# Loading the second half of the token rows into weight and filter buffers, and transposing them among the filter units

## The chip, the cores and the metric

One core of a Trainium2 chip runs the kernel. The metric is the device time of one execution in microseconds (us); the median of three runs of the kernel before is 1380.2 us (1378.26 to 1383.59).

## The reference, cut to what matters

One transformer block on 1024 tokens of width 1024, with a context of 256 tokens. In float32:

```python
x = x + pos_embed
mod_x, mod_c = split(silu(c) @ w_ada + b_ada, 6), split(silu(c_ctx) @ w_ada + b_ada, 6)
def project(h, mod):
    return modulate(rmsnorm(h, norm_mix_g), mod[0], mod[1]) @ w_in   # q, k, v, g, decay gates, hyena inputs
# gated linear attention over the context, then over the tokens, both directions
# hyena: 3-tap convolution, then two long convolutions by FFT with filters made from
#   h = sin(freq * (sin(freq * (z @ w1 + b1)) @ w2 + b2)) @ w3, times a decay
x = x + mod_x[2] * (concat(gla, hyena) @ w_out)
x = x + mod_x[5] * expert_choice_moe(modulate(rmsnorm(x, norm_ffn_g), mod_x[3], mod_x[4]))   # 16 experts
return rmsnorm(x, norm_final_g)
```

The change lies in the beginning: the token rows (`x` plus position embedding, normalised and modulated), the first third of `mod_x`, and the spectra of the hyena filters.

## The kernel before, in words

The kernel is one straight program over five compute engines. Who computes what: TensorE (PE) multiplies, VectorE (DVE) and ScalarE (ACT) do elementwise work, GpSimd (POOL) and SyncE (SP) mostly issue transfers. The source is traced from top to bottom; a planner then sets the order of each engine and each queue. It takes the earliest source line that it reckons to be ready and to have a free buffer, by its own estimate of durations. On the chip each engine and each queue then works strictly in that order, and waits where a needed result or a transfer is later than reckoned.

Buffers are slots shared by tag. The ones that matter here:

- `gen`, 7 slots of 4 KB a partition: the features `zf`, the layers `h1` and `h2`, the split filter weights `w3` (two) and `h2h`, and the token rows `xt`. The last three of the former stay until the filter units are through, so four slots are left for token rows.
- `raw`, 3 slots: raw blocks of `w_in` (`w_block`, L508 to L520) and, later, pieces of `w_ada`.
- `whi` and `wlo`, 3 slots each: the two halves of a split `w_in` block, and before that the two halves `kk` of a filter unit (L453).
- `wa`, 8 slots: the first third of `w_ada`.

The beginning, in the order of the source:

1. Small loads on SP (L207 to L223): `w1`, `zf`, then the three columns `fb` (two biases and the frequency), `w2`, the condition columns, `w3raw`. Two sine layers make `h2` from them (L240 to L255).
2. `rows_of` (L279 to L309) for the first four row tiles of `x`: load, add the position embedding with DVE, sum of squares on ACT (L300, into `jk`), `rsqrt`, scale (L305).
3. `mod_begin` (L318) loads `b_ada` into `mo` with eight small transfers on SP; `mod_piece` (L326) streams 16 tiles `wt` of `w_ada` of 512 KB each and multiplies them; `mod_end` (L338) stores a third with four transfers on POOL. The first third is not stored but transposed into columns `mcol` and `g1` (L347 to L356).
4. Small loads on SP for later stages: `wab` and `pre` (L566 to L572), `cw` and `cb` (L644 to L648).
5. `columns` (L496) transposes four row tiles to `xh` and `xl`, with the modulation applied. L640 does it for the first half of the rows. L641 does all of the second half: `rows_of` with `by_dma`, in which SP loads `xt` and POOL adds the position embedding to it by an accumulating transfer (L288, L290), and then its transposes.
6. The same for the 256 context rows (L732 to L734).
7. `filters` (L476): eight units. `filter_front` multiplies and makes `kk`, with a small load `hb` on POOL (L457); `filter_mid` does the first DFT stage (L461 to L471); `filter_end` does the rest on DVE and stores `d_spec` on POOL (L474). A unit's front runs one unit ahead of its mid. After units 5 and 7 stand `value_rows` 0 and 1, whose `short_conv` (L650) multiplies a `w_in` block with both halves of `xh` and `xl`.
8. Gates, context projection and context states, and then the eight long-convolution slots, each with projections and pieces of `w_ada` among them.

In `rows_of`, the lines that matter most for the change are:

```python
xt = gen([P, D], name="xt")
SY.dma_start(xt, src[j * P:(j + 1) * P, :])
if by_dma:
    G.dma_start(xt, io["c_pos"][j], accum_op=ALU.add)
```

Of the kernel before, what the change touches and what calls it, by code (L numbers as in the profile page):

```python
# [98 lines left out]
def tile_gla_hyena_moe(ctx: ExitStack, tc: tile.TileContext, io: dict, out: bass.AP):  # L99
# [34 lines left out]
    def cload(name, shape, dt=F32, pool=None, src=None):  # L134
        t = (pool or const).tile(shape, dt, name=name)
        SY.dma_start(t, io["c_" + name] if src is None else src)
        return t
# [52 lines left out]
    def gen(shape, dt=F32, name="gen"):  # L190
        return gp.tile(shape, dt, name=name, tag="gen", bufs=7)
# [4 lines left out]
    def raw_tile(shape, name="raw"):  # L196
        return wp.tile(shape, F32, name=name, tag="raw", bufs=3)
# [6 lines left out]
    def twice(src, ap):  # L204
        return bass.AP(tensor=src.tensor, offset=src.offset, ap=ap)

    SY.dma_start(w1, twice(io["hy_w1"], [[DK, 33], [0, 2], [1, DK]]))  # L207
    zf = gen([33, L], name="zf")
    SY.dma_start(zf, io["c_zfeat"])
    for i, nm in enumerate(("hy_b1", "hy_b2", "hy_freq")):  # L210
        SY.dma_start(fb[:, i:i + 1], twice(io[nm], [[0, 2], [1, DK], [1, 1]]))
    SY.dma_start(w2, twice(io["hy_w2"], [[DK, DK], [0, 2], [1, DK]]))
    ccol = early.tile([P, KT, 2], F32, name="ccol")
    SY.dma_start(ccol[:, :, 0], io["c"][0].rearrange("(k p) -> p k", p=P))
# [61 lines left out]
    ident = cload("ident", [P, P])  # L276


    def rows_of(src, h, W, with_pos, by_dma=False):  # L279
        if with_pos and not by_dma:  # L280
            posc = s2([P, 512], name="posc")
            SY.dma_start(posc, io["c_posc"])
        xs_ = []
        ms = tiny.tile([P, W], F32, name="pms")
        for w in range(W):
            j = h * W + w
            xt = gen([P, D], name="xt")
            SY.dma_start(xt, src[j * P:(j + 1) * P, :])  # L288
            if by_dma:
                G.dma_start(xt, io["c_pos"][j], accum_op=ALU.add)  # L290
            elif with_pos:
                pr = s2([P, 512], name="posr")
                for q in range(2):
                    row = io["c_posr"][2 * j + q]
                    SY.dma_start(pr[64 * q:64 * q + 64],
                                 bass.AP(tensor=row.tensor, offset=row.offset, ap=[[0, 64], [1, 512]]))
                V.tensor_add(xt[:, 0:512], xt[:, 0:512], pr)
                V.tensor_add(xt[:, 512:1024], xt[:, 512:1024], posc)
            jk = s2([P, D], BF16, name="jk")
            A.activation(jk, xt, AF.Square, accum_out=ms[:, w:w + 1])  # L300
            xs_.append(xt)
        rs = tiny.tile([P, W], F32, name="prs")
        rsqrt(rs, ms, float(D), W)
        for w in range(W):
            A.activation(xs_[w], xs_[w], AF.Copy, scale=rs[:, w:w + 1])  # L305
        return xs_
# [5 lines left out]

    wav = w_ada.rearrange("(k p) (t h f) -> t k h p f", p=P, h=2, f=1024)

    def mod_columns(rows, t, g):
        return rows[:, 2048 * t:2048 * t + 2048].rearrange("r (h g j) -> r g h j", h=2, g=4)[:, g]

    def mod_begin(t, pool):  # L318
        mo = pool.tile([P, 512], F32, name="mo", tag="mo", bufs=1)
        G.memset(mo, 0.0)  # L320
        for g in range(4):
            for i in range(2):
                SY.dma_start(mo[32 * g + i:32 * g + i + 1].rearrange("r (h j) -> r h j", h=2), mod_columns(io["b_ada"], t, g))
        return mo

    def mod_piece(t, kqs, mo, raw):  # L326
# [9 lines left out]
        return V.tensor_add(mo, pm, mo)  # L336

    def mod_end(t, mo):  # L338
        for g in range(4):
            G.dma_start(mod_columns(d_mod, t, g), mo[32 * g:32 * g + 2].rearrange("r (h j) -> r h j", h=2))  # L340

    mo = mod_begin(0, early)
    mod_piece(0, range(4), mo, lambda shape, name: wap.tile(shape, F32, name=name, tag="wa", bufs=8))
    gcol = early.tile([P, KT], F32, name="gcol")
    SY.dma_start(gcol, io["norm_mix_g"][0].rearrange("(k p) -> p k", p=P))
    mcol = early.tile([P, 2, 2, KT], F32, name="mcol")
# [218 lines left out]

    wab = early.tile([65, NH, 2, DK], F32, name="wab")  # L566
    V.memset(wab, 0.0)
    for d, x in enumerate("fb"):
        for r in (0, 32):
            SY.dma_start(wab[r + 16 * d:r + 16 * d + 16, :, d], io["gla_wa_" + x][0].rearrange("r (h k) -> r h k", h=NH))  # L570
        SY.dma_start(wab[64:65, :, d], io["gla_ba_" + x].rearrange("r (h k) -> r h k", h=NH))
    pre = cload("pre", [P, 2 * (CH + 2)], pool=early)  # L572
    sgn = early.tile([P, 2], F32, name="sgn")
    for x in range(2):
        V.memset(sgn[0:64, x:x + 1], 1.0 - 2.0 * x)
# [62 lines left out]
    xh = [xpool.tile([P, L], F32R, name=f"xh{k}") for k in range(KT)]  # L638
    xl = [xpool.tile([P, L], F32R, name=f"xl{k}") for k in range(KT)]
    columns(first_rows, 0, 0, xh, xl)  # L640
    columns(rows_of(io["x"][0], 1, 4, True, True), 1, 0, xh, xl)  # L641


    cw = early.tile([P, 12, 3], F32, name="cw")  # L644
    for j in range(3):
        SY.dma_start(cw[:, :, j], io["hy_conv_w"][0, j].rearrange("(b p) -> p b", p=P))
    cb = early.tile([P, 12], F32, name="cb")
    SY.dma_start(cb, io["hy_conv_b"][0].rearrange("(b p) -> p b", p=P))  # L648

    def short_conv(b, depth=3):  # L650
        ps = pA([P, L], name="phy")
# [162 lines left out]
    def value_rows(b, depth=3):  # L814
        u = short_conv(b, depth)
        uts[(0, b)] = to_time_rows(lambda n1: u[:, n1::8])

    filters(decay0, {5: lambda: value_rows(0, 2), 7: lambda: value_rows(1, 2)})
    hl = gate_weights()
    context_gates(hl)  # L820
    block_a(hl)
# [626 lines left out]
```

## Time and profile before

| what | value |
| --- | --- |
| median of 3 runs | 1380.2 us |
| the profiled execution, its own time | 1380.59 us |
| its span, first to last instruction | 1378.8 us |
| PE busy | 1276.7 us (93% of the span) |
| DVE busy | 1149.8 us (83%) |
| ACT busy | 805.8 us (58%) |
| POOL busy | 129.9 us (9%) |
| mean granted TensorE clock | 0.964 |
| moved by DMA | 354.81 MB, mean 257 GB/s |

Busy time is an average over stages with different limits, so it says where to look and not what a change is worth. A row of a stage table gives, for one stretch of time, how long each engine was busy in it, the granted clock of TensorE (1.00 is 2.4 GHz, 0.50 is 1.2 GHz) and the share of time in which the 16 DMA engines worked. A row of a timeline gives start, duration, engine, line, and operation, and in brackets how long the engine had been idle and what ended that. SPq is SP's queue of transfers. In a row of the timeline the duration of SPq is the time that issuing takes, not the time until the data is there.

### The profile page before, as it was taken

The numbers are of one execution on the slowest core, as the hardware profiler recorded it, in microseconds if no ns is written. First come the engines' busy times: TensorE is split into PE (matmuls) and PEld (weight loads), VectorE is DVE, ScalarE is ACT, GpSimd is POOL, SyncE is SP. The second block draws the span as 40 slices with busy tenths as digits, with TensorE's granted clock in tenths as the row PEclk, the third lists the DMA queues.
The fourth block names the chain that finished last, engine by engine and source line by source line (L and its number), as shares of the span: only waits on it lengthen the run. The fifth ranks groups of instructions, "written<-read, shape, count | busy, mean of one in ns | idle before, by whom it ended". The sixth has DMA issues, their size and how long they took to land.

```text
span 1378.8 us, 21543 instructions
## 1 busy us (share of the span) xinstructions
PE 1276.7 (93%) x7720; PEld 1044.5 (76%) x7720; DVE 1149.8 (83%) x1920; ACT 805.8 (58%) x1228; POOL 129.9 (9%) x142
## 2 busy tenths in 40 slices
PE   6988999999999998988996899999999999999982
PEld 4777888688898897766775678888888888877762
DVE  6877938899778678788656799999999999988886
ACT  3247453121211314886553678888888888877864
POOL 1020000010100110001000000001111111012010
PEclk9998999999999998999996899999999999999996
DMA  7993551774746545676768789999999999999765
GB/s 213 325 230 123 167 145 42 234 199 150 202 152 185 141 113 176 159 165 186 242 230 337 244 318 357 361 394 383 387 385 386 390 385 391 369 365 370 264 202 225
DMA packets 154362, 354.81 MB, mean 257 GB/s; under 512 B 28389, under 2 KB 74013, under 8 KB 153999
## 3 DMA queue, kind: packets, MB, share of 16 engines
q1 hardware_dynamic: 134911, 292.84, 59.7%
q0 software_dynamic: 19344, 60.61, 15.8%
q8 instruction: 60, 0.98, 0.3%
q14 instruction: 47, 0.39, 0.1%
HBM read 310.89 MB, written 50.89 MB: 262 GB/s over the span
## 4 chain that ended last, share of the span: by engine, by line
PE 70%; issue 9%; DMA 7%; DVE 7%; ACT 5%; POOL 1%; SPq 1%; POOLq 0%; DVEq 0%; ACTq 0%
PE pex L151 13%; PE pex L152 12%; PE pex L150 12%; PE phy L543 3%; PE phy L542 3%; PE phy L545 3%; PE ptx L1343 2%; PE pdft L467 2%; PE pdft L468 2%; PE pvg L150 2%; PE pm L334 2%; PE pvg L152 1%; PE pvg L151 1%; PE pdft L671 1%; DMA wt<-w_ada 1%
## 5 line engine op out<-in xcount | busy, mean ns | idle before, releaser
L147 DVE TENSOR_TENSOR elo<-eraw,ehi 128x1024 fp32r<-128x1024 f32 x256 | 302.5, 1221 | 13.2 <-issue 6.0
L151 PE MATMUL pex<-elo,thi 128*128 128x512 f32 x768 | 306.4, 399 | 4.8 <-DVE elo L147 4.4
L150 PE MATMUL pex<-ehi,thi 128*128 128x512 f32 x768 | 305.8, 398 | 2.3 <-ACT thi L144 1.3
L152 PE MATMUL pex<-ehi,tlo 128*128 128x512 f32 x768 | 303.4, 395 | 0.8 <-DVE tlo L147 0.8
L144 ACT ACTIVATE ehi<-eraw 128x1024 fp32r<-128x1024 f32 x256 | 265.0, 1068 | 50.2 <-PE pex L152 49.3
L151 PEld LDWEIGHTS pex<-elo,thi 128*128 128x128 f32 x768 | 145.3, 189 | 40.3 <-DVE elo L147 10.5
L150 PEld LDWEIGHTS pex<-ehi,thi 128*128 128x128 f32 x768 | 145.3, 189 | 33.9 <-ACT thi L144 1.7
L152 PEld LDWEIGHTS pex<-ehi,tlo 128*128 128x128 f32 x768 | 145.3, 189 | 31.6 <-DVE tlo L147 1.2
L147 DVE TENSOR_TENSOR elo<-erawl,ehi 128x1024 fp32r<-128x1024 f32 x128 | 149.5, 1221 | 6.2 <-ACT ehi L144 5.3
L144 ACT ACTIVATE ehi<-erawl 128x1024 fp32r<-128x1024 f32 x128 | 131.3, 1057 | 19.6 <-PE pex L152 17.4
L144 ACT ACTIVATE whi<-wraw 128x1024 fp32r<-128x1024 f32 x30 | 31.8, 1059 | 104.6 <-DMA wraw<-w_in 29.6
L542 PE MATMUL phy<-xh,whi 128*128 128x512 f32 x192 | 77.2, 402 | 12.2 <-ACT whi L144 12.2
L543 PE MATMUL phy<-xl,whi 128*128 128x512 f32 x192 | 76.1, 396 | 0.0
L150 PE MATMUL pvg<-whi,xh 128*128 128x256 f32 x256 | 73.3, 286 | 0.0
L151 PE MATMUL pvg<-wlo,xh 128*128 128x256 f32 x256 | 72.5, 283 | 0.0
L152 PE MATMUL pvg<-whi,xl 128*128 128x256 f32 x256 | 72.5, 283 | 0.0
L1389 POOL DMA_INDIRECT d_acc<-y,ix x15 | 34.6, 2308 | 392.4 <-DVE y L1388 392.4
L1348 ACT ACTIVATE tt<-ptx,fcol,gfcol 128x128 f32<-128x128 f32 x128 | 48.7, 463 | 34.1 <-PE ptx L1343 34.1
L545 PE MATMUL phy<-xh,wlo 128*128 128x512 f32 x192 | 61.9, 400 | 0.0
L438 ACT ACTIVATE D<-pdft 128x512 f32<-128x512 f32 x32 | 19.1, 597 | 70.9 <-PE pdft L468 40.7
L147 DVE TENSOR_TENSOR wlo<-wraw,whi 128x1024 fp32r<-128x1024 f32 x30 | 36.7, 1222 | 22.5 <-ACT whi L144 22.5
L467 PE MATMUL pdft<-kk,fmat 128*128 128x128 f32 x256 | 52.7, 289 | 0.3 <-ACT D L438 0.2
(452 smaller groups left out, 2601.1 us busy)
## 6 DMA issues: line engine op xcount, KB each, us to landing
eraw<-w_gate SPq DMA_DIRECT2D x128, 512.0 KB
eraw<-w_up SPq DMA_DIRECT2D x128, 512.0 KB
erawl<-w_down SPq DMA_DIRECT2D x128, 512.0 KB
wt<-w_ada SPq DMA_DIRECT2D x48, 512.0 KB
wraw<-w_in SPq DMA_DIRECT2D x30, 512.0 KB
kspec<-d_spec SPq DMA_DIRECT2D x16, 512.0 KB
xt<-x SPq DMA_DIRECT2D x8, 512.0 KB
d_spec<-ue POOLq DMA_DIRECT2D x8, 512.0 KB, 6.0
```

The lines of the kernel that those rows point to most:

```text
L144: A.activation(hi, src, AF.Copy)
L147: V.tensor_sub(lo, src, hi.bitcast(F32))
L150: T.matmul(out_, lh, rh, start=first, stop=False)
L151: T.matmul(out_, lh, rl, start=False, stop=False)
L152: T.matmul(out_, ll, rh, start=False, stop=last)
L334: T.matmul(pm[32 * g:32 * g + 32, 256 * h:256 * h + 256], sc[:, k], wt[:, 256 * g:256 * g + 256], start=k == ks[0] and h == 0, stop=k == k ...
L467: T.matmul(ps[:, r], fmat[:, r, m1], kk[m1 // 4][:, 0, m1 % 4], start=True, stop=False)
L542: T.matmul(ps[:, h], hi[:, k], rh[k][:, h], start=k == 0, stop=False)
L543: T.matmul(ps[:, h], hi[:, k], rl[k][:, h], start=False, stop=False)
L545: T.matmul(ps[:, h], lo[:, k], rh[k][:, h], start=False, stop=k == KT - 1)
L1348: A.activation(tt[:, k], pt[:, k], AF.Identity, bias=fcol[:, 0, kk_:kk_ + 1], scale=gfcol[:, kk_:kk_ + 1])
L1389: G.indirect_dma_start(out=d_acc[:, :], out_offset=bass.IndirectOffsetOnAxis(ap=ix[:, :1], axis=0), in_=y, in_offset=None, compute_op=ALU.add)
```

## The change

Five edits:

- The three `fb` loads are issued by ACT, ahead of all others, and no longer by SP.
- `b_ada` is loaded in two transfers for each third and not eight; a third of the modulation is stored in two transfers and not four.
- Row tiles 4 and 5 (`early_rows`) are loaded into two `raw` slots, by SP right behind the `w_ada` stream, and their position embedding is added by POOL's accumulating transfer at that place in the source.
- Row tiles 6 and 7 are loaded into one `whi` and one `wlo` slot, after filter unit 3 in the source (`second_rows`), with the statistics and the scaling of all four. Their transposes (`second_columns`) stand after unit 4. `value_rows(0)` moves from after unit 5 to after unit 6.
- The small loads `cw`, `cb`, `wab` and `pre` are issued behind the loads of row tiles 6 and 7.

```diff
+    for i, nm in enumerate(("hy_b1", "hy_b2", "hy_freq")):
+        A.dma_start(fb[:, i:i + 1], twice(io[nm], [[0, 2], [1, DK], [1, 1]]))
     SY.dma_start(w1, twice(io["hy_w1"], [[DK, 33], [0, 2], [1, DK]]))
     zf = gen([33, L], name="zf")
     SY.dma_start(zf, io["c_zfeat"])
-    for i, nm in enumerate(("hy_b1", "hy_b2", "hy_freq")):
-        SY.dma_start(fb[:, i:i + 1], twice(io[nm], [[0, 2], [1, DK], [1, 1]]))
...
-    def rows_of(src, h, W, with_pos, by_dma=False):
+    def rows_of(src, h, W, with_pos, by_dma=False, tiles=None, done=0):
...
-            xt = gen([P, D], name="xt")
-            SY.dma_start(xt, src[j * P:(j + 1) * P, :])
-            if by_dma:
+            xt = tiles[w]() if tiles else gen([P, D], name="xt")
+            if w >= done:
+                SY.dma_start(xt, src[j * P:(j + 1) * P, :])
+            if by_dma and w >= done:
                 G.dma_start(xt, io["c_pos"][j], accum_op=ALU.add)
-            elif with_pos:
+            elif with_pos and not by_dma:
...
-        for g in range(4):
-            for i in range(2):
-                SY.dma_start(mo[32 * g + i:32 * g + i + 1].rearrange("r (h j) -> r h j", h=2), mod_columns(io["b_ada"], t, g))
+        for i in range(2):
+            SY.dma_start(mo[i::32].rearrange("g (h j) -> g h j", h=2), mod_columns(io["b_ada"], t, 0))
...
     mod_piece(0, range(4), mo, lambda shape, name: wap.tile(shape, F32, name=name, tag="wa", bufs=8))
+    early_rows = []
+    for w in range(2):
+        early_rows.append(raw_tile([P, D], name="xt"))
+        SY.dma_start(early_rows[w], io["x"][0][(4 + w) * P:(5 + w) * P, :])
+        G.dma_start(early_rows[w], io["c_pos"][4 + w], accum_op=ALU.add)
...
     columns(first_rows, 0, 0, xh, xl)
-    columns(rows_of(io["x"][0], 1, 4, True, True), 1, 0, xh, xl)
+    second = []
+    def second_rows():
+        late = [lambda t=t: wp.tile([P, D], F32, name="xt", tag=t, bufs=3) for t in ("whi", "wlo")]
+        second.append(rows_of(io["x"][0], 1, 4, True, True, [lambda w=w: early_rows[w] for w in range(2)] + late, 2))
+        small_loads()
+    def second_columns():
+        columns(second[0], 1, 0, xh, xl)
...
-    filters(decay0, {5: lambda: value_rows(0, 2), 7: lambda: value_rows(1, 2)})
+    filters(decay0, {3: second_rows, 4: second_columns, 6: lambda: value_rows(0, 2), 7: lambda: value_rows(1, 2)})
```

## Rows read from the trace of the kernel before

**Rows 1.** Stage table: stretch, its length, PE PEld DVE ACT POOL busy, clock, DMA

```profile
28.00:96.90 68.90, 68.80 (x606) 59.32 (x605) 57.26 (x123) 25.43 (x42) 11.51 (x19) 1.00 0.84 262
...
113.30:160.00 46.70, 46.45 (x310) 41.30 (x309) 41.22 (x89) 32.81 (x56) 2.66 (x5) 1.00 0.45 138
96.90:160.00 63.10, 50.70 (x326) 45.25 (x326) 48.78 (x108) 37.95 (x67) 3.19 (x6) 0.89 0.52 153
160.00:200.00 40.00, 39.71 (x259) 32.98 (x257) 20.17 (x31) 19.04 (x32) 2.16 (x4) 1.00 0.60 173
```

**Rows 2.** Stage table of the hole and what follows it, same columns

```profile
96.90:102.00 5.10, 0.11 (x1) 0.00 (x0) 2.57 (x5) 1.22 (x3) 0.00 (x0) 0.77 1.06 253
102.00:109.10 7.10, 0.00 (x0) 0.00 (x0) 0.91 (x4) 3.24 (x6) 0.00 (x0) 0.50 0.69 200
109.10:113.30 4.20, 4.14 (x17) 3.95 (x18) 4.08 (x12) 0.68 (x4) 0.54 (x1) 0.50 0.31 125
```

**Rows 3.** Timeline of ACT and PE, 95 to 110 us

```profile
95.82 1.06 ACT L300 ACTIVATE jk<-xt 128x1024 bf16<-128x1024 f32 x1 [5.68 <-DMA xt<-c_pos]
...
107.01 1.06 ACT L300 ACTIVATE jk<-xt 128x1024 bf16<-128x1024 f32 x1 [2.51 <-DMA xt<-c_pos]
...
108.07 1.04 ACT L144 ACTIVATE whi<-wraw 128x1024 fp32r<-128x1024 f32 x1
...
109.16 0.79 PE L542 MATMUL phy<-xh,whi 128*128 128x512 f32 x1 [12.15 <-ACT whi L144]
```

**Rows 4.** Timeline of SP and POOL, 73 to 93 us

```profile
73.09 2.65 SPq L516 DMA_DIRECT2D wraw<-w_in  x3
83.93 1.85 SPq L288 DMA_DIRECT2D xt<-x  x4
...
88.22 0.90 POOL L290 DMA_DIRECT2D xt<-c_pos  x1 [8.99 <-DMA xt<-x]
...
92.65 0.86 POOL L290 DMA_DIRECT2D xt<-c_pos  x1 [0.33 <-PE pw L452]
```

**Rows 5.** Instructions on tile `xt`: from issue to landing of the accumulating transfers

```profile
DMA to landing us min/median/max: 7.5/11.4/14.3
```

**Rows 6.** Timeline of SP, DVE and ACT, 0 to 33 us

```profile
0.74 0.42 SPq L207 DMA_DIRECT2D w<-hy_w  x1
...
1.59 1.23 SPq L211 DMA_DIRECT2D fb<-hy_b  x2
2.86 1.79 SPq L211 DMA_DIRECT2D fb<-hy_freq  x1
...
27.49 3.49 SPq L323 DMA_DIRECT2D mo<-b_ada  x4
...
8.80 0.15 DVE L224 TENSOR_SCALAR fb<-fb 128x1 f32<-128x1 f32 x1 [5.67 <-DMA fb<-hy_freq]
...
0.75 1.28 ACT L1359 ACT_TABLE_LOAD   x1 [0.75 <-PEq L1438]
...
10.09 0.22 ACT L227 ACTIVATE sc<-ccol 128x16 f32<-128x16 f32 x1 [8.05 <-DMA ccol<-c_ctx]
...
13.48 1.06 ACT L247 ACTIVATE w<-w3raw 128x1024 fp32r<-128x1024 f32 x1 [0.72 <-DMA w3raw<-hy_w]
14.44 0.61 ACT L236 ACTIVATE h<-sy 64x512 f32<-64x512 f32 x1
```

**Rows 7.** Timeline of PE: the last products of filter units 2 and 3

```profile
63.71 0.39 PE L468 MATMUL pdft<-kk,fneg 128*128 128x128 f32 x2
...
79.52 0.39 PE L468 MATMUL pdft<-kk,fneg 128*128 128x128 f32 x2
```

**Rows 8.** Chain of waits, start and duration: one wait for a `w_in` block

```profile
264.04 5.85 DMA wraw<-w_in
```

**Rows 9.** Instructions on tile `hb`: from issue to landing

```profile
DMA to landing us min/median/max: 2.4/4.4/14.2
```

**Rows 10.** Instructions on `d_spec`: from issue to landing

```profile
DMA to landing us min/median/max: 2.9/5.2/12.5
```

More of the change, by code (lines that the diff above doesn't have):

```diff
@@ L313, in tile_gla_hyena_moe, with mod_columns @@
     wav = w_ada.rearrange("(k p) (t h f) -> t k h p f", p=P, h=2, f=1024)
-    def mod_columns(rows, t, g):
-        return rows[:, 2048 * t:2048 * t + 2048].rearrange("r (h g j) -> r g h j", h=2, g=4)[:, g]
+    def mod_columns(rows, t, i):
+        return rows[i, 2048 * t:2048 * t + 2048].rearrange("(h g j) -> g h j", h=2, g=4)
     def mod_begin(t, pool):
@@ L338, in mod_end @@
     def mod_end(t, mo):
-        for g in range(4):
-            G.dma_start(mod_columns(d_mod, t, g), mo[32 * g:32 * g + 2].rearrange("r (h j) -> r h j", h=2))
+        for i in range(2):
+            G.dma_start(mod_columns(d_mod, t, i), mo[i::32].rearrange("g (h j) -> g h j", h=2))
     mo = mod_begin(0, early)
     mod_piece(0, range(4), mo, lambda shape, name: wap.tile(shape, F32, name=name, tag="wa", bufs=8))
+    early_rows = []
[3 more added lines that the diff above has]
+        G.dma_start(early_rows[w], io["c_pos"][4 + w], accum_op=ALU.add)
     gcol = early.tile([P, KT], F32, name="gcol")
@@ L567, in tile_gla_hyena_moe @@
     V.memset(wab, 0.0)
[L568 to L572, printed above, removed]
+    pre = early.tile([P, 2 * (CH + 2)], F32, name="pre")
     sgn = early.tile([P, 2], F32, name="sgn")
@@ L640, in tile_gla_hyena_moe, with small_loads @@
     columns(first_rows, 0, 0, xh, xl)
-    columns(rows_of(io["x"][0], 1, 4, True, True), 1, 0, xh, xl)
+    second = []
[5 more added lines that the diff above has]
+        columns(second[0], 1, 0, xh, xl)
     cw = early.tile([P, 12, 3], F32, name="cw")
-    for j in range(3):
-        SY.dma_start(cw[:, :, j], io["hy_conv_w"][0, j].rearrange("(b p) -> p b", p=P))
     cb = early.tile([P, 12], F32, name="cb")
-    SY.dma_start(cb, io["hy_conv_b"][0].rearrange("(b p) -> p b", p=P))
+    def small_loads():
+        for j in range(3):
+            SY.dma_start(cw[:, :, j], io["hy_conv_w"][0, j].rearrange("(b p) -> p b", p=P))
+        SY.dma_start(cb, io["hy_conv_b"][0].rearrange("(b p) -> p b", p=P))
+        for d, x in enumerate("fb"):
+            for r in (0, 32):
+                SY.dma_start(wab[r + 16 * d:r + 16 * d + 16, :, d], io["gla_wa_" + x][0].rearrange("r (h k) -> r h k", h=NH))
+            SY.dma_start(wab[64:65, :, d], io["gla_ba_" + x].rearrange("r (h k) -> r h k", h=NH))
+        SY.dma_start(pre, io["c_pre"])
     def short_conv(b, depth=3):
```

## Prediction, made before the changed kernel was run

> **What bounds the kernel now.** I read the stage tables first. From 28 to 96.9 us PE is busy without a gap, and again from 113.3 to 200 us [rows 1]. So what shortens another engine's work there gains nothing, and only time in which PE stands idle or runs slowly can be won. Between the two lies a hole: PE does 0.11 us of work in 12.2 us, and the 4.14 us of work behind the hole run at a granted clock of 0.50, that is at 1.2 GHz, where the stretches on either side have 1.00 [rows 1, 2].
>
> Then the timeline says who ends the hole. PE waits 12.15 us for ACT's split of the first `w_in` block, `whi` [rows 3]. That block was asked for at 73 us [rows 4]; it is not late. ACT is: in its fixed order the split stands behind the four sums of squares `jk` of the second half of the rows, and each of these waits for an accumulating transfer of the position embedding. The last ends its wait at 107.01, the split starts at 108.07, PE at 109.16 [rows 3]. Behind PE's waiting product stand the remaining filter units, which need nothing of it.
>
> Then I followed the rows back. Their loads are issued at 83.93, when the first half has left its `gen` slots; POOL issues the first accumulation at 88.22 and the last at 92.65 [rows 4]; these land 7.5 to 14.3 us later [rows 5]. So the second half is late because it waits for slots that another tag could have given.
>
> **The change part by part.** The sum is made against the profiled execution, 1380.6 us, which is 0.4 us above the median of the runs.
>
> *Rows 4 and 5 early.* Two loads on SP and two accumulations on POOL move from 84 to 93 us to behind the `w_ada` stream. They take no new transfer time. Ahead of them on SP stand the 16 `w_ada` loads, behind them the small loads; on POOL, stores of spectra and `hb`. PE has filter units and modulation products to do in that time, 68.80 of 68.90 us [rows 1], which is the cover. If it is gone, the cost is that of the rival on POOL's queue below.
>
> *Rows 6 and 7 in `whi` and `wlo`.* Their slots come free when a filter unit's last product has read `kk`: unit 2 ends at 63.7 us, unit 3 at 79.5 [rows 7]. From issue to the first accumulation took 4.3 us (83.93 to 88.22), the loads 1.85 us [rows 4], the landing 7.5 to 14.3 [rows 5]. Asked for behind unit 2, they are ready between 63.7 + 4.3 + 7.5 = 75.5 and 63.7 + 1.9 + 4.3 + 14.3 = 84.2 us; behind unit 3, between 91.3 and 100.0. I take unit 2, since with three slots a tag the source asks for the tile when units 3 and 4 hold two and unit 2 has left the third. Either way two slots remain for the filters, one in use and one being filled, so I cost that at nothing: PE's other unit covers it.
>
> *The hole.* With the rows ready by 84 us, ACT has no reason to stand, and PE's filter units 5 to 7 lie behind the transposes as work that needs no row. I take the whole idle time, 5.10 − 0.11 + 7.10 = 12.1 us, as won, and with it the slow stretch: 4.14 us of work at half the clock lose 4.14 / 2 = 2.1 us [rows 2]. Bounds: from nothing to 14.2.
>
> *What is late next.* DVE. In 96.9 to 160 us it works 48.8 of 63.1 us; with 14.2 us gone it would have 48.9, so it would have to run without a gap. In 113.3 to 160 it reaches 41.22 / 46.70 = 88% [rows 1]. At 88% its 48.8 us need 55.3, which is 6.4 more than there is. But DVE has half of 160 to 200 us free, 20.17 of 40 [rows 1], and the later filter units' spectra are not wanted before the convolutions. So between 0 and 6.4 us are given back; I take 2, nearer to the free row.
>
> *`fb` on ACT.* SP loses three issues, 1.23 + 1.79 = 3.0 us, all ahead of what it loads next. But `fb` itself has only 1.59 − 0.74 = 0.85 us of issues ahead of it on SP [rows 6], so the first sine layer, which starts when `fb` lands at 8.80, comes at most 0.85 us sooner. If ACT's table load of 1.28 us stands ahead of the three issues, it comes 0.4 us later. The second part of the layer leaves ACT at 14.44, behind a split that waited for `w3raw` until 13.48 [rows 6]; that load comes 3 us earlier. ACT is idle until 10.09 otherwise, which hides the issues. So the beginning wins between −0.4 and 3.0 us; I take 1.3, between the 0.85 of `fb` and the 1.6 that `h` waits for the split and behind it.
>
> *`b_ada` in two transfers.* Four issues cost SP 3.49 us [rows 6]; six fewer spare some 5 us of SP ahead of the `w_ada` stream. PE is full by then, so nothing is won. The four stores less for each later third spare POOL issues on an engine that is busy 11.5 of 68.9 us [rows 1]: nothing.
>
> *Two `raw` slots held.* Three `w_in` blocks were asked for at 73 us [rows 4]; now one can be, and the others when the transposes are through. The second block is wanted only after the first block's products. Lower bound nothing, upper one wait as seen later, 5.9 us [rows 8]. I take nothing, as filter units lie beside it.
>
> *Small loads moved behind.* `cw` and `cb` are wanted at the first `short_conv`, `wab` and `pre` later still; nothing, with some 20 us between.
>
> Sum: 1380.6 − 12.1 − 2.1 + 2.0 − 1.3 = 1367.1 us. The rest of the program hangs on PE, so I expect it to move up by the same amount.
>
> One rule was weighed. The accumulations landed after 7.5 to 14.3 us [rows 5]. The Trainium skill's page "DMA: Bandwidth & Descriptors" (section "Anatomy of one DMA — SWDGE (gpsimd) path") gives a transfer issued by GpSimd about 2.0 us and its bytes at 436 GB/s, an estimate of 3.2 us for 512 KB. This trace does not agree; the measurement decides. By that rule of the Trainium skill even rows asked for behind unit 3 would be ready by 90 us, before the hole, and the first rival below would give 1367 as well.
>
> **The rivals.**
>
> *Half the hole stays.* Rows 6 and 7 are asked for behind unit 3, and are ready at 91.3 to 100.0 us. Then come two squares, `rsqrt` and the scaling, and ACT stands before other work as it does now. For it: the source puts the request behind unit 3. Against it: the slot is free earlier. With 6 us of hole left, the clock falls again (it had gone to 0.50 within the 12 us [rows 2]): 1380.6 − 1.3 − 6.1 = 1373.2 us.
>
> *The change doesn't do what it says.* The planner gives the free `whi` and `wlo` slots to units 5 to 7 first, and the late tiles get theirs no earlier than 84 us, as now. Only the beginning is won: 1379.3 us.
>
> *Slower: POOL's queue.* The accumulations now share POOL's queue with `hb` and the spectra's stores while PE is full, and `hb` is needed before the next unit's products. `hb` lands after 4.4 us in the median, but once took 14.2 us [rows 9]. If two pairs of accumulations each hold up one `hb` by 14.2 − 2.4 = 11.8 us beyond its slack, PE loses 23.6 us and, with the clock down after each, 2 × 2.1 more: 1367.1 + 27.8 = 1394.9. It decides the sign when the two stalls together pass 13.5 us. Against it: `hb` is asked for a unit ahead, and unit 2 to unit 3 takes 15.8 us [rows 7]. The Trainium skill's page "SBUF — State Buffer" (section "SBUF: two separate sides") speaks for it: transfers issued by GpSimd starve while VectorE runs in a fast mode on two ports, and DVE is busier where they go. The stores of spectra, as large and on the same queue, landed there after 5.2 us in the median [rows 10], which does not look starved, and so I give it little.
>
> **How the numbers follow.** Forecast 0.62, half the hole 0.20, nothing but the beginning 0.10, POOL's queue 0.08. The forecast's own bounds: best 1380.6 − 14.2 − 3.0 = 1363.4; worst 1380.6 − 14.2 + 6.4 + 0.4 = 1373.2. Single runs spread by some 2.5 us about the median, so the range goes down to 1361. Upward it takes in the half hole and most of its spread, to 1377; what is left out is the third and fourth case, 18 in 100. About 0.5%, 6.9 us, is what a measurement of this kernel can tell from no change: faster means below 1373.3, slower above 1387.1. Faster has the forecast but for a little, 0.60, and half of the first rival, 0.10, together 0.70; the same 0.22; slower 0.08. The likeliest case gives 1367 us.
>
> **What would show it.** Right: the wait of PE for `whi` is gone and the clock stays at 1.00 from 40 to 200 us; the last accumulation lands before PE's unit 4 ends; the transposes of the second half run among the filter units; DVE is above 90% up to 150 us; every later stage starts some 13 us earlier. The first `fb` operation of DVE before 8.8 us and the first DFT product some 1.3 us earlier would show the beginning. Wrong: ACT still waiting for `xt<-c_pos` with evictions of the DFT behind it (half the hole); the late tiles' loads issued after 80 us (the third case); DVE waiting for `hb` or for a store's slot (POOL's queue); PE waiting for the second `w_in` block. The forecast falls as a whole if the time won by 200 us is given back later, in the convolution slots or before the experts, by an order of the planner that I can't foresee.

## The result, and the profile after

The changed kernel takes 1390.8 us in the median of four runs, the kernel before 1379.2 beside it: a ratio of 1.0074 (95% interval 1.0053 to 1.0095). It is some 10 us slower where 1367 us was forecast. Both the range and the sign were wrong. The profiled execution, the slowest of the four, has a span of 1391.7 us against 1378.8, 12.9 us more.

Where the 12.9 us come from is seen by the first start of the same product in both traces. The first filter product `pw` starts 2.5 us later (23.2 against 20.7), the first context-gate product `pga` 10.8 us later (171.5 against 160.7), the first expert product 12.9 us later. So 11 us are lost before 172 us. The other 2 appear between 180 and 400 us; 1.4 of them are PE waiting longer for pieces of `w_ada` (2.5 us instead of 1.1 between 160 and 420 us), the rest was not followed up.

The stage table says how they are lost. First the kernel before, in two windows that the rows ahead of the prediction don't have (columns as in [rows 1]: window, length, then busy us and count of PE, PEld, DVE, ACT and POOL, granted clock, DMA share, GB/s):

```profile
28.00:160.00 132.00, 119.50 (x931) 104.57 (x931) 106.04 (x231) 63.38 (x108) 14.70 (x25) 0.95 0.69 210
80.00:140.00 60.00, 47.50 (x339) 43.72 (x338) 45.89 (x101) 37.31 (x65) 7.30 (x11) 0.89 0.59 173
```

And the kernel after: the same windows, and the three stretches in which its clock is low.

```profile
28.00:160.00 132.00, 116.89 (x886) 102.52 (x885) 105.24 (x233) 61.83 (x105) 15.74 (x27) 0.94 0.68 211
80.00:140.00 60.00, 46.85 (x323) 43.79 (x322) 46.26 (x106) 38.73 (x71) 3.87 (x8) 0.86 0.49 148
...
85.20:88.60 3.40, 3.40 (x18) 3.40 (x18) 1.68 (x3) 0.00 (x0) 0.00 (x0) 0.52 1.04 299
92.10:98.90 6.80, 6.18 (x30) 6.18 (x31) 6.52 (x19) 3.05 (x6) 0.56 (x1) 0.52 0.20 78
109.10:116.00 6.90, 5.84 (x28) 5.85 (x29) 6.03 (x19) 4.36 (x8) 0.54 (x1) 0.52 0.06 23
```

PE stands idle 132 − 116.89 = 15.1 us where it stood 12.5. And its clock falls to about 1.2 GHz three times instead of once, each time behind a wait for `D`: 15.4 us of work at 0.52 lose 7.4 us, where 4.14 at 0.50 lost 2.1 [rows 2]. Together: 2.5 at the start, 2.6 of idle time, 5.3 of clock, 10.4 of the 10.8 us by which the gates are late. Half of the loss is clock.

The one hole of 12 us [rows 3] has not been filled but cut in pieces. PE's longest waits in 80 to 160 us (us in total, times, longest):

```profile
PE pdft L472 <- ACT D L443: 11.4, 5, 4.6
PE phy L550 <- DVE wlo L147: 1.3, 1, 1.3
...
```

`whi` is gone from the list, as forecast. In its place PE waits for `D`, ACT's eviction of a DFT product, and ACT's own timeline shows what stands ahead of `D`:

```profile
83.54 0.63 ACT L443 ACTIVATE D<-pdft 128x512 f32<-128x512 f32 x1
88.85 1.06 ACT L301 ACTIVATE jk<-xt 128x1024 bf16<-128x1024 f32 x1 [4.69 <-DMA xt<-ctx]
...
91.03 1.06 ACT L301 ACTIVATE jk<-xt 128x1024 bf16<-128x1024 f32 x1 [1.03 <-DMA xt<-ctx]
...
92.09 0.58 ACT L443 ACTIVATE D<-pdft 128x512 f32<-128x512 f32 x1
...
108.48 1.05 ACT L301 ACTIVATE jk<-xt 128x1024 bf16<-128x1024 f32 x1
...
109.52 0.58 ACT L443 ACTIVATE D<-pdft 128x512 f32<-128x512 f32 x1
```

The squares at 88.85 and 91.03 are those of the **context** rows, which the prediction never mentions. In the source they are traced ahead of the filters; the second half now comes inside the filters, so the planner puts the context first. The second half's own squares, whose last accumulation was issued at 79.24, run at 105 to 109 without a wait: its rows lay ready, and ACT had not come to them.

The context loads are late because of what stands ahead of them on SP. After, then before (start, us of issuing, transfer):

```profile
58.96 9.41 SPq L660 DMA_DIRECT2D cw<-hy_conv_w  x3
68.42 0.70 SPq L661 DMA_DIRECT2D cb<-hy_conv_b  x1
...
70.55 1.05 SPq L289 DMA_DIRECT2D xt<-x  x2
...
80.67 0.88 SPq L289 DMA_DIRECT2D xt<-ctx  x2
```

```profile
68.39 2.46 SPq L646 DMA_DIRECT2D cw<-hy_conv_w  x3
70.90 2.14 SPq L648 DMA_DIRECT2D cb<-hy_conv_b  x1
```

`cw` and `cb` are read in single elements of four bytes. Before, only `w_in` blocks stood behind them on SP, which nobody missed. After, the planner puts them ahead of the two late rows, though the source has them behind, and 5671 of the 6459 packets from 58 to 70 us are under 512 bytes. The Trainium skill's page "DMA: Bandwidth & Descriptors" (section "Rules for kernel authors") says that a last dimension that is not contiguous becomes one descriptor per element; the trace agrees with it, by that count.

The start is seen in three views of the kernel after: DVE's first operation on `fb`, ACT's issues, and SP's waits.

```profile
11.90 0.15 DVE L224 TENSOR_SCALAR fb<-fb 128x1 f32<-128x1 f32 x1 [8.77 <-DMA fb<-hy_freq]
```

```profile
0.74 1.68 ACTq L208 DMA_DIRECT2D fb<-hy_b  x2
2.45 0.68 ACTq L208 DMA_DIRECT2D fb<-hy_freq  x1
```

```profile
SPq L136 <- DMA fb<-hy_freq: 2.6, 1, 2.6
SPq L222 <- DMA fb<-hy_b: 2.4, 2, 1.8
```

`fb` is issued by 3.13 us instead of 4.65 and lands 3.1 us later than in [rows 6], and the profile puts 5.0 us of waiting on SP, which was to be relieved, down to these loads.

### The profile page after: what moved, and what is told of

It is laid out like the page before. It is cut to its first block, busy times and chain, and to the rows that moved or that the text cites. A ratio compares the mean times of both kernels' runs of the same rounds, so it can differ in the third digit from the quotient of the medians.

```text
span 1391.7 us, 21494 instructions
## 1 busy us (share of the span) xinstructions
PE 1282.2 (92%) x7720; PEld 1048.6 (75%) x7720; DVE 1149.6 (83%) x1920; ACT 806.1 (58%) x1228; POOL 128.0 (9%) x138
## 4 chain that ended last, share of the span: by engine, by line
PE 67%; issue 9%; DVE 8%; DMA 7%; ACT 6%; SPq 1%; POOL 1%; POOLq 0%; ACTq 0%; DVEq 0%
PE pex L151 13%; PE pex L152 12%; PE pex L150 12%; PE phy L550 3%; PE phy L548 3%; PE phy L547 3%; PE ptx L1361 2%; DMA wt<-w_ada 2%; PE pvg L150 2%; PE pvg L151 1%; PE pvg L152 1%; PE pdft L689 1%; PE pdft L472 1%; PE pdft L473 1%; PE py L713 1%
## 5 line engine op out<-in xcount | busy, mean ns | idle before, releaser
L472 PE MATMUL pdft<-kk,fmat 128*128 128x128 f32 x256 | 55.7, 303 | 11.5 <-ACT D L443 11.4
L472 PEld LDWEIGHTS pdft<-kk,fmat 128*128 128x128 f32 x256 | 43.8, 213 | 15.8 <-ACT D L443 12.7
## 6 DMA issues: line engine op xcount, KB each, us to landing
eraw<-w_gate SPq DMA_DIRECT2D x128, 512.0 KB, 11.1
```

The lines of the kernel that those rows point to most:

```text
L472: T.matmul(ps[:, r], fmat[:, r, m1], kk[m1 // 4][:, 0, m1 % 4], start=True, stop=False)
```

## The experiments

Every ratio is to the kernel before, run beside it. "Idle" is PE's idle time from 28 to 160 us, "clock" the granted clock there, "gates" the start of the first context-gate product. Where two intervals overlap by much, the time does not tell the two versions apart: e5, e6 and e7 from e3, e10 from the changed kernel, e14 and e16 from e9.

| run | ratio (95% interval) | idle, us | clock | gates, us |
|---|---|---|---|---|
| before | 1 | 12.5 | 0.95 | 160.7 |
| after | 1.0074 (1.0053 to 1.0095) | 15.1 | 0.94 | 171.5 |
| e1_fb_sp | 1.0122 (1.0105 to 1.0140) | 21.5 | 0.95 | 172.8 |
| e2_ctx_behind | 1.0032 (1.0015 to 1.0049) | 9.7 | 0.99 | 160.2 |
| e3_fb_sp_ctx | 1.0009 (0.9997 to 1.0021) | 12.4 | 0.99 | 159.7 |
| e4_before_fb_act | 1.0036 (1.0023 to 1.0049) | 11.8 | 0.97 | 163.7 |
| e5_small_late | 1.0014 (1.0003 to 1.0025) | 14.9 | 0.97 | 164.9 |
| e6_values_first | 1.0017 (1.0006 to 1.0028) | 9.3 | 0.96 | 162.2 |
| e7_rows_by_2 | 1.0018 (1.0007 to 1.0029) | 12.4 | 0.96 | 162.2 |
| e8_spectra_copied | 0.9983 (0.9968 to 0.9998) | 9.4 | 0.97 | 158.1 |
| e9_hold | 0.9987 (0.9973 to 1.0000) | 11.2 | 1.00 | 156.8 |
| e10_after_hold | 1.0060 (1.0038 to 1.0082) | 14.4 | 0.95 | 165.8 |
| e11_vals_hold | 1.0006 (0.9991 to 1.0020) | 9.0 | 0.97 | 160.4 |
| e12_before_b_ada | 1.0049 (1.0029 to 1.0068) | 15.9 | 0.94 | 167.2 |
| e13_after_old_bada | 1.0109 (1.0090 to 1.0128) | 19.8 | 0.91 | 176.1 |
| e14_hold_old_bada | 0.9973 (0.9962 to 0.9984) | 7.9 | 0.99 | 155.5 |
| e15_hold_copies | 0.9963 (0.9948 to 0.9979) | 7.1 | 1.00 | 153.1 |
| e16_hold_pool | 0.9996 (0.9981 to 1.0010) | 10.1 | 0.97 | 160.9 |
| e17_ctx_last | 1.0118 (1.0098 to 1.0139) | 10.8 | 0.99 | 175.7 |
| e18_ctx_last_values | 1.0117 (1.0098 to 1.0137) | 9.8 | 0.95 | 176.9 |

**`fb` and the context.** In e1 the `fb` loads go back to SP:

```
-    for i, nm in enumerate(("hy_b1", "hy_b2", "hy_freq")):
-        A.dma_start(fb[:, i:i + 1], ...)
     SY.dma_start(zf, io["c_zfeat"])
+    for i, nm in enumerate(("hy_b1", "hy_b2", "hy_freq")):
+        SY.dma_start(fb[:, i:i + 1], ...)
```

> The changed kernel with its three fb loads back on SP behind zf. Theory (the loads on ACT start the sine layers later): DVE's first fb operation goes back from 11.90 to about 8.8 us, the first pw product from 23.2 to about 20.7, and the whole kernel is 2.5 to 2.8 us shorter than the changed one, 1388 us. Rival (the start is absorbed: PE is full from 28 us on, and what comes earlier waits in front of the same DFT evictions): the start is 2.8 us earlier and the end within 1 us of 1390.8.

The start came back (`fb` at 8.78, `pw` at 20.7), and the kernel is slower than the changed one all the same, by 0.5%. The gain is not only absorbed, it is turned round: the context loads now go out at 84.88 instead of 80.67, and ACT stands 8.87 us for them instead of 4.69.

```profile
91.23 1.06 ACT L301 ACTIVATE jk<-xt 128x1024 bf16<-128x1024 f32 x1 [8.87 <-DMA xt<-ctx]
```

So neither the gain of the theory nor the unchanged time of the rival came out. What grew with the loss is ACT's wait for the context rows, which e2 takes away.

For e2 the context columns are traced behind filter unit 5:

```
-    columns(rows_of(io["ctx"][0], 0, NTC, False), 0, 1, ch, cl)
+    def context_columns():
+        columns(rows_of(io["ctx"][0], 0, NTC, False), 0, 1, ch, cl)
...
-    filters(decay0, {3: second_rows, 4: second_columns, 6: ...
+    filters(decay0, {3: second_rows, 4: second_columns, 5: context_columns, 6: ...
```

> The changed kernel with the context rows (their loads, squares, scaling and transposes) traced behind the second half's transposes, so that ACT's order takes the second half first. Theory (ACT stands at squares that wait for context rows asked for at 80.7 us, and DFT evictions and the second half's ready rows stand behind them): PE's holes at 92.7, 110.2 and 127.8 us (3.0, 4.6, 1.5 us) go or shrink below 1.5 us each, the clock stays at 1.00 from 40 to 120 us but for one dip at most, and the kernel takes 1390.8 - 5 to - 12 = 1379 to 1386 us. Rival (it is the number of ACT's evictions, squares, scalings and splits between 74 and 125 us, whatever their order): the holes move by some us, their sum stays at 9 to 15 us between 80 and 160 us, and the time stays within 2 us of 1390.8. Second rival (held slots of raw, whi and wlo delay the filter units or the first w_in blocks): the same time as the changed kernel, and PE waiting for whi or wlo longer than 5 us.

The theory held: 5.8 us back (1.0074 to 1.0032), no hole over 1.9 us, clock 0.99. No work was taken out; only the order changed. PE's longest wait for `wlo` is 1.8 us and it has none for `whi`, so the held slots, the second rival, are not it. e3 has both edits.

> Both edits: fb back on SP and the context rows behind the second half. If both theories hold, the sum of the two gains: 1390.8 - 2.7 - 5 to - 12 = 1376 to 1383 us, 1379 of the kernel before being inside that. If only the first half's evictions and transposes count (the hole at 84 us), about 1386.

It is level with the kernel before. In this order `fb` on SP is worth 0.0023, 3 us, about what the start lost, though the two intervals overlap a little. What keeps it from the forecast of 1367 shows in SP, POOL and ACT:

```profile
65.44 9.18 SPq L660 DMA_DIRECT2D cw<-hy_conv_w  x3
74.72 1.72 SPq L289 DMA_DIRECT2D xt<-x  x1
```

```profile
83.26 0.87 POOL L291 DMA_DIRECT2D xt<-c_pos  x1 [7.35 <-DMA wab<-gla_wa_f]
```

```profile
88.96 1.06 ACT L301 ACTIVATE jk<-xt 128x1024 bf16<-128x1024 f32 x1 [4.16 <-DMA xt<-c_pos]
```

The last late row is asked for behind `cw`, its accumulation goes out at 83.26, and ACT stands again, with `D` behind it.

e4 is the kernel before with `fb` on ACT, the first edit of the change alone.

> The kernel before with one part of the change alone: the three fb loads on ACT ahead of w1. Theory: 2.5 to 2.8 us slower than before, 1382 us, with DVE's first fb operation at about 11.9 us instead of 8.8. Rival (prediction of the change): 1.3 us faster, 1378, fb at 8.0. Second rival: the start is late, but the hole before the second half's rows, which waits on SP and POOL, takes it up, and the end is within 0.7 us of before.

Slower by 0.23 to 0.49%, 3 to 7 us, with `fb` at 12.00: the prediction's sign is wrong, and the hole does not take the delay up.

**The small loads, and where the first block stands.** e5 to e7 move calls in the source of e3:

```
     def second_rows():
         ...
-        small_loads()
     def second_columns():
         columns(second[0], 1, 0, xh, xl)
+        small_loads()
```

> The kernel of e3_fb_sp_ctx (1381.6 us) with the small loads (cw, cb, wab, pre) called behind the second half's transposes instead of with its rows. In e3 the planner put the three cw loads (9.18 us on SP, 65.44 to 74.6) between the two late row loads, the last late accumulation is issued at 83.26 and ACT's fourth square waits 4.16 us for it, to 88.96. Theory (small loads in front of the last row): the last late load is issued by 70, its square runs by 84, PE's waits at 81 and 91 us (2.88 + 2.34) shrink by 3 us or more, 1378 us. Rival (DVE sets the pace of 80 to 140 us, where it is busy 56.65 of 60): the rows come sooner, DVE stays at 94% or more, and the time is within 1.5 us of 1381.6.

This settled nothing: SP issues `cw` at 66.97 for 9.35 us, ahead of the last row, as in e3. The planner put these loads, which depend on nothing, in the same place though the source has them later.

```
+    filters(decay0, {3: second_rows, 4: second_columns, 5: lambda: value_rows(0, 2), 6: context_columns, 7: lambda: value_rows(1, 2)})
```

> As e5, and the first convolution block (value_rows) traced behind unit 5 and the context rows behind unit 6, so that PE has w_in products to do beside the DFT units, as before. Theory (in 80 to 140 us DVE's filter work is the bound and PE has nothing else to do; the kernel before did 12 us of phy products in 109 to 140): phy begins before 112 us instead of 119.6, PE's idle time of 28 to 160 us falls from 12.2 to about 7, 1376 us. Rival (ACT's evictions): phy earlier, idle time within 1.5 us of e5's, and the time the same as e5's.

`phy` begins at 115.3 and the idle time is the least so far, 9.3, but the clock is 0.96, and the time is that of e5. e7 is e6 with `{2: second_rows, 3: second_columns, ...}`.

> As e6, and the late rows asked for behind unit 2 instead of 3, their transposes behind unit 3. If the late rows' slots set when the second half is ready: the last accumulation is issued before 72 us and phy begins some 8 us sooner than in e6, up to 4 us off the time. If the tags lent from whi and wlo are then short for the units: PE waits for kk or w longer, and 2 to 5 us slower than e6.

The slots were not what was late: the two loads go out at 56.04, the last accumulation by 74. This run all but fulfils the prediction's condition, rows ready by 84 us: the four squares run from 81.79 to 85.98 without waiting for a transfer. PE stands 7.39 us all the same, for `D`:

```profile
81.79 1.08 ACT L301 ACTIVATE jk<-xt 128x1024 bf16<-128x1024 f32 x1
...
84.91 1.07 ACT L301 ACTIVATE jk<-xt 128x1024 bf16<-128x1024 f32 x1
...
85.94 0.61 ACT L443 ACTIVATE D<-pdft 128x512 f32<-128x512 f32 x1
```

```profile
86.61 0.80 PE L472 MATMUL pdft<-kk,fmat 128*128 128x128 f32 x2 [7.39 <-ACT D L443]
```

ACT does not wait here; it works. From the first half's columns it goes straight to four squares, and the eviction that PE needs has its turn behind them.

Since e5 could not move the small loads, e9 to e11 hold them by a dependency, three short DVE operations:

```
     def small_loads():
+        last = second[0][3]
+        V.tensor_copy(cw.rearrange("p b j -> p (b j)"), last[:, 0:36])
+        V.tensor_copy(cb, last[:, 0:12])
+        V.tensor_scalar(wab.rearrange("p h d k -> p (h d k)"), last[0:65, 0:512], 0.0, None, op0=ALU.mult)
```

> The kernel of e3_fb_sp_ctx (1381.6 us) with the small loads (cw, cb, wab) held until the second half's rows are scaled, by three short DVE operations that write their tiles from a scaled row. In e3 the three cw loads take SP 9.18 us between the two late row loads (before: 2.46 us at 68.39, with no row load in front or behind), and in 60 to 90 us the DMA engines are 90% busy at 212 GB/s. Theory (the small loads in their new place stand in front of the last row): the last late accumulation is issued before 75 us instead of 83.26, ACT's wait of 4.16 us for it at 88.96 is gone, PE's idle time of 80 to 97 us falls from 3.9 to below 2, time 1376 to 1379 us. Rival (the late rows' slots or POOL's queue): the last accumulation is issued after 80 us all the same, and the time stays within 1.5 us of 1381.6.

The theory is right in direction: 0.0022 less than e3, 3 us, with intervals that overlap a little. SP asks for the last row at 66.55 to 71.4, the accumulation goes out at 79.80 (not before 75, as expected), and ACT's wait shrinks from 4.16 to 2.58. `cw`, now at 97.62, is issued in 2.33 us.

```profile
66.55 4.84 SPq L289 DMA_DIRECT2D xt<-x  x1
...
97.62 2.33 SPq L663 DMA_DIRECT2D cw<-hy_conv_w  x3
```

```profile
87.42 1.06 ACT L301 ACTIVATE jk<-xt 128x1024 bf16<-128x1024 f32 x1 [2.58 <-DMA xt<-c_pos]
```

e10 is the same hold in the changed kernel.

> The changed kernel (1390.8 us) with the same hold on the small loads and nothing else. Theory: the context loads are issued right behind the second half's, before 78 us instead of 80.67, ACT's waits for them (4.69 and 1.03 us) shrink, and the time falls by 2 to 6 us; the context squares still run ahead of the second half, so not to before's time. Rival (only the order on ACT counts): within 1.5 us of 1390.8.

The context loads go out at 78.34, ACT waits 1.91 and 2.01 us for them instead of 4.69 and 1.03, and the ratio is 0.0014 lower, 2 us. That is the low end of the theory, and the intervals overlap, so by time alone it is open; the gates come 5.7 us earlier.

> The kernel of e9 with the first convolution block traced behind unit 5 and the context rows behind unit 6. If late rows and a late first block are the two causes that are left: phy begins by 110 us, idle time of PE in 28 to 160 us below 6 us, and 1373 to 1377 us, below the kernel before. If ACT's and DVE's sum of work between 70 and 125 us is the bound, the holes move to other evictions and the time stays at 1379 to 1383 us.

The second answer, as far as the time tells: 1.0006 against 0.9987, 2.6 us slower than e9, with intervals that overlap a little. `phy` is earlier (112.5 against 118.3), with less idle time and a lower clock.

**The edit that was costed at nothing.** e12 is the kernel before with the `b_ada` edit alone, as in the diff of `mod_columns`, `mod_begin` and `mod_end`; e13 and e14 undo it in the changed kernel and in e9.

> The kernel before with the b_ada edit alone: two transfers for eight in each third, two stores for four. Prediction: nothing. Theory (w_ada's stream starts some 5 us sooner, PE takes the modulation products earlier and DFT units later, and the first half's transposes come 4 us sooner): the first modulation product at about 38 us instead of 46.3, the transposes at 70 to 72 instead of 76.2; the second half's loads with them, 80 instead of 83.93; the time within 3 us of before, on either side.

It costs 0.49%, 6.8 us, more than expected. The `w_ada` loads are all issued by 54.25 us instead of 60.09, and the second half is asked for at 78.54. PE's order now has DFT products ahead of the first `phy`, and ACT's has `D` behind three of the second half's squares, which wait for accumulations. PE stands 14.1 us in four waits for `D`. The longest, 9.07 us, is in the place of the 12.15 for `whi` [rows 3]; the next, 4.03 us, is new, and there `D` stands behind the second half's columns and the two context squares:

```profile
99.83 0.58 PE L466 MATMUL pdft<-kk,fmat 128*128 128x128 f32 x1 [9.07 <-ACT D L437]
```

```profile
125.97 0.80 PE L466 MATMUL pdft<-kk,fmat 128*128 128x128 f32 x2 [4.03 <-ACT D L437]
```

> The changed kernel (1390.8 us) with the b_ada edit undone: eight transfers and four stores in each third, as before. Theory (an earlier w_ada stream lets the modulation products displace DFT units before 70 us, and these are then done when ACT and DVE are the bound): the first half's transposes go back from 72.65 to about 76 us, and the time falls by 3 to 6 us. Rival (additive costs were an accident of the order in e12): the time within 2 us of 1390.8.

The transposes went back (77.1 us), the time did not: 0.0035 more than the changed kernel. `cb` takes 8.16 us on SP, the context is asked for only at 96.02, and ACT stands for it longest of all:

```profile
100.06 1.06 ACT L301 ACTIVATE jk<-xt 128x1024 bf16<-128x1024 f32 x1 [11.16 <-DMA xt<-ctx]
```

e10, after, e1 and e13 ask for the context at 78.3, 80.7, 84.9 and 96.0 us, and ACT's first wait for it is 1.9, 4.7, 8.9 and 11.2.

> The kernel of e9 (1378.9 us) with the b_ada edit undone. Theory: more DFT units before 70 us, DVE busier in 28 to 80 us (before 41.2 us, in e9 39.5), so less of its work in 80 to 140: PE's idle time of 28 to 160 us falls from 11 us to 8, 1375 to 1377 us. Rival (the row loads now come later by as much): idle time the same, time within 1.5 us of e9.

The mechanism is as expected: 41.6 us of DVE's work in 28 to 80 us instead of 39.5, and 7.9 us of idle time instead of 11.2. The time is 0.0014 below e9, 2 us, which the intervals do not tell from nothing. At 0.9973 (0.9962 to 0.9984) it is, of the versions that leave nothing out, the only one that is clear of the kernel before: 3.7 us below it and 14 below the change.

**What is left.** e8 and e15 leave out most of the second DFT stage in four units, in e3 and in e9:

```
-        for q, u in enumerate(dft8(*sd)):
+        if (o, g) in ((1, 1), (0, 2), (1, 2), (0, 3)):
+            outs = []
+            for q, name in ((0, "ue"), (1, "uo")):
+                u = cv([P, 4, 2, C], name=name)
+                V.tensor_copy(u, sd[q])
+                outs.append(u)
+        else:
+            outs = dft8(*sd)
+        for q, u in enumerate(outs):
```

> The kernel of e3_fb_sp_ctx with the second stage of the DFT left out in the spectra of four filter units (the fourth to the seventh): two copies instead of some 18 DVE operations, about 6 us of DVE less a unit. It leaves that part of the filters out. Theory (DVE is the bound of 80 to 140 us): PE's idle time of 28 to 160 us falls from 12.2 us to below 7 and the time by 5 us or more, to 1376 or less. Rival (ACT's order: late rows and evictions behind squares and splits): DVE's busy share falls, PE's idle time stays within 2 us, and the time within 2 us of 1381.6.

> The kernel of e9 (1378.9 us) with the second DFT stage of four filter units left out as in e8: DVE has some 24 us less to do in 80 to 160 us. If DVE is the bound in e9: PE's idle time of 80 to 140 us falls from 9 us to 4 or less, and the time to 1374 or less. If ACT's order is (columns of the first half up to 80 us, then squares in front of the evictions): PE's holes at 81, 103 and 108 us stay as long as they are, and the time within 2 us of e9.

Neither theory has it all. e8 gains 3.6 us on e3, e15 3.3 on e9. The stage rows of e9, then of e15:

```profile
80.00:140.00 60.00, 50.92 (x378) 46.25 (x379) 58.51 (x137) 37.00 (x68) 6.00 (x11) 1.00 0.59 165
```

```profile
80.00:140.00 60.00, 53.60 (x406) 49.90 (x407) 45.90 (x91) 40.97 (x73) 7.17 (x10) 1.00 0.63 178
```

With DVE busy 97.5% in e9 and 76.5% in e15, PE's idle time falls from 9.1 to 6.4 us only. What stays in e15 are mostly two evictions behind columns, of the first half at 82 us and of the second at 109:

```profile
PE pdft L472 <- ACT D L443: 5.6, 3, 2.9
PE pw L456 <- DVE kk L459: 0.9, 1, 0.9
```

e16 gives four of the `xl` subtractions to POOL (`eng=G if h == 1 and k % 2 else None` in `split`).

> The kernel of e9 (1378.9 us) with four of the eight subtractions that make xl in the second half's columns (0.68 us each on DVE) on POOL. If DVE is the bound: 1 to 3 us faster. If POOL's operation takes several times DVE's, the s2 slots come free later, and ACT's columns stall behind it: 1 to 4 us slower. If ACT's order is the bound: within 1 us.

No gain; 1.2 us to the worse, inside the intervals. POOL takes 1962 ns in the mean for what takes DVE 0.68 us:

```profile
L147 POOL TENSOR_TENSOR xl<-tt,xh 128x512 fp32r<-128x512 f32 x4 | 7.8, 1962 | 1.3 <-ACT xh L144 1.3
```

In e14 both engines are full where PE stands longest (ACT 12.34 and DVE 13.00 of 13 us):

```profile
97.00:110.00 13.00, 9.63 (x77) 8.46 (x76) 13.00 (x29) 12.34 (x20) 0.53 (x1) 1.00 0.49 74
```

So e17 and e18 move the context rows behind all units, `context_columns()` on a line of its own behind `filters(...)`; e18 also has `value_rows(0, 2)` at 5.

> The kernel of e14 (1376.9 us) with the context rows' squares, scaling and columns traced behind all eight filter units. They take ACT some 9 us and DVE 3.4 us between 109 and 131 us in e14. If the two engines' sum of work in 80 to 140 us is the bound: PE's idle time there falls by 1 to 4 us and the time to 1373 to 1376. If the planner puts them back among the units, or the context gates then wait for them: the same as e14 or up to 2 us slower.

> As e17, and the first convolution block traced behind unit 5 as in the kernel before. If PE lacks work that needs neither ACT nor DVE: phy begins before 112 us (e14: 115.4) and another 1 to 2 us are gained. If DVE's pace sets the end of the units whatever lies beside them (as e11 against e9, 2.3 us slower): 1 to 3 us slower than e17.

Both lose 20 us on e14. In e17 SP asks for the context at 156.22, behind two `w_in` blocks whose issue holds SP 10.69 us, and PE waits:

```profile
PE pt L507 <- ACT xt L306: 7.1, 2, 6.7
```

From 80 to 140 us ACT's work fell from 41.59 to 31.94 us, and PE's grew from 52.08 to 52.40 only. So it is not the context's share of the work that holds PE up in that stretch.

## Why the prediction was wrong

**The hole.** The step that failed is "With the rows ready by 84 us, ACT has no reason to stand, and PE's filter units 5 to 7 lie behind the transposes as work that needs no row". Its diagnosis was right: ACT's fixed order stands at squares, and PE waits behind it. The cure was not. ACT stood next at the context squares (4.69 us), which the step "what is late next" left out; e2 shows this, as the order alone gives 5.8 us back. And the filter units need no row, but they do need ACT: every other DFT product is evicted as `D` in the same fixed order. So "which need nothing of it", said of the units behind the first `w_in` block, was true of the block and not of ACT's queue. In e7 the rows are ready and ACT waits for no transfer ahead of that `D`, yet PE stands 7.39 us behind columns and squares. For the second half ACT works some 18 us (in e14 the squares take it from 85.98 to 90.14, the scalings 4.26 us, the columns from 99.52 to 108.99), with the 9.5 us of the first half's columns just ahead. In the kernel before, a part of that lay inside the hole [rows 3], and so did the eviction. There too `D` stands behind all four squares and the split:

```profile
109.11 0.58 ACT L438 ACTIVATE D<-pdft 128x512 f32<-128x512 f32 x1
```

The DFT products share two buffers. PE had filled both by 97.01 us, and this eviction frees the first at 109.69; without the wait for `whi` the next DFT product would, in this order of ACT, have waited for `D` as long. e12, where PE's order has the DFT products first, shows such a wait, 9.07 us. So the hole was never 12.1 us of waiting that could simply be taken out. And the clock, counted as 2.1 us to win, cost 5.3 more, as it fell behind three shorter waits.

**The small loads.** "Nothing, with some 20 us between" looked at who needs `cw` and `cb`, not at who is queued behind them, and took the order of the source for that of the queue. They cost the late rows, and by these the context, their place on SP; e9 against e3 puts 3 us on it. The rows were counted as asked for at 63.7 us; with `cw` in front they went out at 70.55, and the last accumulation at 79.24. That unit 2 was taken rather than unit 3 decided nothing: in e7 both late rows are asked for at 56.04, and the time is no better.

**`fb` on ACT.** A gain of 1.3 was forecast, from −0.4 to 3.0. It lost 2.5 to 2.7 us at the start (`pw` at 23.2 and 23.3 in after and e4, at 20.7 and 20.5 in before and e3), outside those bounds. At the end e4 puts 3 to 7 us on it, e3 against e2 3. The bound took the landing time as fixed and counted issues only.

**`b_ada`.** Forecast nothing; alone it cost 6.8 us, and undoing it in e9 won 2 that the intervals don't separate from nothing. "PE is full by then" was true and did not decide: what changed is which work PE is full of, modulation products or DFT units, and so what is left for the stretch in which ACT and DVE are short (DVE's 39.5 and 41.6 us before 80 us in e9 and e14). Its price depends on the order around it: undone in the changed kernel it made things worse.

**DVE.** 2 us were to be given back, up to 6.4. DVE did rise to 97.5% once the order was mended (e9), and what e8 and e15 took off it won 3 to 4 us. Mechanism and range were right for that order; in the changed kernel itself it was not reached: DVE there has 46.3 of 60 us.

**The rest.** POOL's queue, the rival on the slower side, is not what happened: no wait of DVE or PE from 20 to 180 us names `hb` or a store. It had the sign, not the mechanism. Its accumulations landed after 8.2 us in the median, two kinds of store beside them, from 58 to 70 us, after 3.4 and 6.4. The Trainium skill's page "SBUF — State Buffer" (section "SBUF: two separate sides"), which has GpSimd's transfers starve while VectorE runs in a fast mode, can be neither confirmed nor refuted here, as no trace names the mode. In e9, with DVE busy 97.5% of 80 to 140 us, POOL's stores landed after 3.1 and 3.2 us in the median. Of PE's waits only the 1.3 us for `wlo` can point at the held slots, near the nothing that was forecast. The move of `value_rows(0)` had no term in the sum; with it moved back, e6 against e5 and e11 against e9 show no gain. That the rest moves by the same amount is true within 2 us: gates 10.8 later, end 12.9; in e14 gates 5.2 earlier, end 4.8.

Not settled: why the planner's order puts DFT products ahead of the first `phy` in e12 and behind it in the kernel before, and the context squares ahead of a `D` that PE wants. It follows from estimates that no run here shows. And part of PE's idle time stays in every version, 7.9 us in e14 with both ACT and DVE full in its worst stretch.

## What to carry to other kernels

Before a wait on an in-order engine is costed as time to be won, list what else that engine serves in the same stretch. If the work that is to fill the hole must be evicted by the engine that stands, the hole moves and does not close. An edit on a queue is priced by what stands behind it there, not by when its own data is wanted; and where the order is fixed by a planner, each part of a change has to be run alone: here `fb` and `b_ada` cost 5 and 7 us one by one, the whole change 10, and undoing either of them in it made things worse.

## What was unexpected of the hardware

Moving three loads of 128 four-byte elements to another engine's queue made them land 3.1 us later, and SP's waits of 5.0 us are put down to them. In that kernel the `ccol` loads, also of four bytes, leave SP at 2.36 instead of 6.39 and so run beside `fb`; whether that is the cause was not tried. The Trainium skill's page "DMA: Bandwidth & Descriptors" (section "Issuing engines are not separate DMA queues") has transfers of all issuing engines run on the same 16 DMA engines, so that another queue saves issue time only. This trace agrees on the issue time, 1.5 us won; the 3.1 us lost in landing is what the trace shows beside it.

The same three `cw` loads, 6 KB each, took SP between 2.1 us (at 99.78 in e14) and 11.1 us (at 62.44 in e7) to issue. In e14 no row load was in flight beside them.

The clock did not follow the idle time alone. In e9 PE had holes of 2.9, 1.3, 1.5 and 1.8 us between 80 and 140 us, and the granted clock of that stretch is 1.00; in the changed kernel it was 0.52 from 85.2 us on, behind a hole of 1.8 us that ended at 84.22.
